# The u blocks of the experts taken in pairs, VectorE in written order, GpSimd's low part behind VectorE's

## The chip, the cores and the metric

The kernel runs on one core of one Trainium2 chip. The metric is the device time of one execution in microseconds. Before the change it is 2007.62 us, the median of 3 runs (2006.73 to 2009.07).

## The reference

Two transformer blocks on a sequence of 256 tokens of width 1024, all in float32: a gated delta net and a sliding-window attention, each with a convolutional MLP, then a block of a conformer convolution beside windowed attention, and last a product-key expert layer, which is what the change touches:

```python
def chunk_fn(hc):
    q = (hc @ w_query).reshape(TOKEN_CHUNK, PEER_HEADS, 2, PEER_HALF)
    sc = jnp.einsum('thpd,pnd->thpn', q, sub_keys).astype(jnp.float32)
    vals, idx = lax.top_k(sc, PEER_TOPK)
    cand = vals[:, :, 0, :, None] + vals[:, :, 1, None, :]
    cand_idx = idx[:, :, 0, :, None] * N_KEYS + idx[:, :, 1, None, :]
    ...
    top_s, pos = lax.top_k(cand, PEER_TOPK)
    expert_idx = jnp.take_along_axis(cand_idx, pos, axis=-1)
    gate = jax.nn.softmax(top_s, axis=-1)
    u = expert_u[expert_idx]
    act = jax.nn.gelu(jnp.einsum('thkd,td->thk', u, hc).astype(jnp.float32), approximate=False)
    vv = expert_v[expert_idx]
    return jnp.einsum('thk,thkd->td', (gate * act).astype(hc.dtype), vv)
```

There are 8 heads, 128 x 128 experts and 16 chosen experts for each head and token.

## The kernel before

The kernel doesn't gather experts. It multiplies all 16384 rows of `expert_u` with the 256 tokens, applies gelu, multiplies by a gate that is zero for experts a token did not choose, and multiplies with all of `expert_v`. The rows come in 128 blocks j of 128 rows, two of which make a pair.

One u block (L973 to L987) goes through all engines. SyncE issues four loads of 128 KB into `raw` (L976, three buffers); the rows come so arranged that VectorE's transpose by 32 x 32 squares (L978) turns the whole 128 x 1024 block into `rt` (two buffers). ScalarE rounds it to the type that TensorE multiplies at full speed: the high part `wh` (L981). The rest, `rt` - `wh`, is the low part `wl` (L223, called through `self.low`). TensorE makes 24 products of 128 x 128 by 128 x 256: for each of 8 k the high part with the tokens' high part, the high part with the tokens' low part, the low part with the tokens' high part (L239 to L241). After two blocks ScalarE writes the gelu of both (L992).

`self.low` gives a low part to VectorE (D) or GpSimd (P) by a table with a row for each stage of the kernel and a counter that runs through all of them (L85, L219 to L223): in the stage "top" the row is PPPD, in "up" PD.

The expert layer has four stages:

- **"top"**, 32 pairs (j < 64, results in `bufa`). Between them run the 8 query heads (projection and scores), the top-k of each head on VectorE (L867 to L884: MAX, MAX_INDEX, MATCH_REPLACE, the candidate sums `cand`), and the tables that turn chosen indices into key numbers and gates (L926 to L930 the selection sums `eq`, and around them).
- **"up"**, 32 pairs (j >= 64, results in `bufb`). After each pair come the gates of 8 tokens for `bufa` (L1044 to L1065): VectorE makes two pairs of one-hot operands, `ga` (L1053) and `gc` (L1056), each 128 x 512, TensorE multiplies them in 16 small products (L1062), and VectorE multiplies `bufa` by the result, which lies in PSUM (L1065). Once in 64 tokens VectorE makes the one-hot rows that `ga` and `gc` are made from (L1019 to L1040).
- **"down"** and **"last"**: the v blocks, with the gates for `bufb` in "down".

The order of instructions on each engine isn't that of the code: a scheduler, which simulates a timeline while the program is built, sets it, and each engine then works through its row in order. So in "up" VectorE's transposes, gate operands and low parts stand as the scheduler placed them.

Two helpers of the residual ahead of the expert layer matter below: `colsum` (L312 to L322), which sums squares over the rows on TensorE (L319) from the tile `rsq`, and `rcol` (L324, L328), which makes the inverse root of them on VectorE and GpSimd; `rrow` (L332 to L340) spreads that over a row tile, taken from the pool `sp`.

Of the kernel before, what the change touches and what calls it, by code (L numbers as in the profile page):

```python
# [86 lines left out]

class Net:
# [867 lines left out]
    def peer(self):  # L956
        nc, tc, I, t = self.nc, self.tc, self.I, self.t
        J0 = 64
        u_rows = I["peer_u_2"][0].rearrange("(j eb ee) (a f) -> j a ee eb f", j=P, ee=32, a=4)
        v_rows = I["peer_v_2"][0].rearrange("(j i) d -> j i d", j=P)  # L960
        xh, xl = self.pq
        tile_ = dict(reuse_waits="tile")
        with tc.tile_pool(name="ba", bufs=1, **tile_) as ba, tc.tile_pool(name="us", bufs=3, **tile_) as us, \
                tc.tile_pool(name="gp", bufs=1, **tile_) as gp, ExitStack() as late:
            bufa = t(ba, [P, J0, T], "bufa")
# [7 lines left out]
            def u_block(j, ps):  # L973
# [4 lines left out]
                nc.vector.transpose(rt, raw)  # L978
                rv = rt.rearrange("p (b f e) -> p f b e", b=4, f=DB)
                uh = t(us, [P, DB, P], "wh", F32R)  # L980
                nc.scalar.copy(uh.rearrange("p f (b e) -> p f b e", b=4), rv)  # L981
                ul = t(us, [P, DB, P], "wl", F32R)
                self.low(ul.rearrange("p f (b e) -> p f b e", b=4), rv,
                         uh.bitcast(F32).rearrange("p f (b e) -> p f b e", b=4))
                for k in range(DB):
                    self.mm3(ps, uh[:, k, :], ul[:, k, :], xh[:, k, :], xl[:, k, :], k == 0, k == DB - 1)

            def u_pair(j, buf):
                ps = self.ps("pp")
                for i in range(2):  # L990
                    u_block(j + i, ps[:, i * T : (i + 1) * T])
                nc.scalar.activation(buf[:, j % J0 : j % J0 + 2, :], ps.rearrange("p (j t) -> p j t", j=2), AF.Gelu)  # L992

            self.wide, self.nwide = True, NW[1]
# [1 line left out]
            with tc.tile_pool(name="kp", bufs=2, side="right", **tile_) as kp:  # L996
                sk = t(kp, [P, 2, P], "sk", bufs=1)
                nc.scalar.dma_start(sk, I["peer_sub_keys_2"][0].rearrange("p n d -> n p d"))
                ps = self.ps()
                for p in range(2):  # L1000
# [9 lines left out]
                          T=lambda i: self.peer_tables(kp, st, i), u=lambda j: u_pair(2 * j, bufa))  # L1010
            self.xq.close()
            bufb = t(late.enter_context(tc.tile_pool(name="bb", bufs=1, side="right", **tile_)),
                     [P, P - J0, T], "bufb")

            N = 64

            def one_hot(t0, lo):

                tk = slice(t0, t0 + N)

                def eq(out, n0, n, key):
                    nc.vector.tensor_tensor(out.rearrange("k n (g t) -> k n g t", t=4),
                                            iot[:, n0 : n0 + n].unsqueeze(2).to_broadcast([P, n, N // 4, 4]),
                                            key[:, tk].rearrange("k (g t) -> k g t", t=4).unsqueeze(1)
                                            .to_broadcast([P, n, N // 4, 4]), op=ALU.is_equal)
# [3 lines left out]
                nc.vector.tensor_tensor(a8, a8, two[:, tk].unsqueeze(1).to_broadcast([P, 8, N]), op=ALU.mult)  # L1031
# [11 lines left out]
            def gates(t0, lo, buf, bank):  # L1043


                if t0 % N == 0:
                    hot["rows"] = one_hot(t0, lo)
                a8, a16, c8, c16 = hot["rows"]
                ps = self.ps(bank)
                for t4 in (0, 4):  # L1050
                    tk = slice(t0 % N + t4, t0 % N + t4 + 4)
                    a = t(gp, [P, 8, 16, 4], "ga", BF16, bufs=2)
                    nc.vector.tensor_tensor(a, a8[:, :, tk].unsqueeze(2).to_broadcast([P, 8, 16, 4]),  # L1053
                                            a16[:, :, tk].unsqueeze(1).to_broadcast([P, 8, 16, 4]), op=ALU.mult)
                    c = t(gp, [P, 8, 16, 4], "gc", F16, bufs=2)
                    nc.vector.tensor_tensor(c, c8[:, :, tk].unsqueeze(2).to_broadcast([P, 8, 16, 4]),  # L1056
                                            c16[:, :, tk].unsqueeze(1).to_broadcast([P, 8, 16, 4]), op=ALU.mult)
                    av = a.rearrange("k h l t -> k (h l) t")
                    cv = c.rearrange("k (j g) l t -> k g j l t", g=2)
                    for i in range(4):  # L1060
                        for g in range(2):
                            nc.tensor.matmul(ps[:, (t4 + i) * 64 : (t4 + i + 1) * 64], av[:, :, i], cv[:, g, :, :, i],  # L1062
                                             start=g == 0, stop=g == 1)
                o = buf[:, :, t0 : t0 + 8]
                nc.vector.tensor_tensor(o, ps.rearrange("p (t j) -> p j t", t=8), o, op=ALU.mult)  # L1065
# [429 lines left out]
```

## Time and profile before

| what | value |
|---|---|
| median of 3 runs | 2007.62 us |
| the profiled execution | 2006.97 us |
| its span, first to last instruction | 2005.2 us |
| TensorE (PE) busy | 1867.5 us, 93% |
| VectorE (DVE) busy | 1464.4 us, 73% |
| ScalarE (ACT) busy | 958.3 us, 48% |
| GpSimd (POOL) busy | 709.2 us, 35% |
| DMA, mean | 153 GB/s |
| low parts of u blocks on GpSimd | 80, 203.2 us |
| first and last gelu of "top" start | 1143.2, 1376.1 us |
| first and last gelu of "up" start | 1381.8, 1608.6 us |

The profile is of one execution. An engine's busy time is that of its instructions, without register, branch and semaphore instructions; a busy TensorE isn't one at its peak, as its products are pipelined and overlap. In a group of instructions, out<-in are the names of tiles. The idle time that stands with an instruction or a group is that of its engine just before it, with what ended it.

### The profile page before, as it was taken

The page shows a single profiled execution, that of the slowest core. Times are in us where ns is not written, and L with a number is a line of the kernel's source. Part 1 is how long each engine was busy: PE and PEld are TensorE (multiplying, and loading weights), DVE is VectorE, ACT ScalarE, POOL GpSimd, SP SyncE. Part 2 cuts the span into 40 slices and gives each one's busy share as a digit, 9 for nine tenths or more (in the row PEclk, how much of TensorE's full clock was granted, in tenths as well). Part 3 has the DMA queues.
Part 4 walks back from the last instruction along what each step waited for, and adds up shares of the span by engine and source line. Part 5 has one row for each costly group of instructions (what it writes and reads, how often), then busy time and mean ns, then how long its engine had stood idle before and what let it go on. Part 6 is the DMA issues. An engine that isn't in the chain of part 4 may idle for free. (4 is left out here: it accounts for less than half of the span.)

```text
span 2005.2 us, 36808 instructions
## 1 busy us (share of the span) xinstructions
PE 1867.5 (93%) x14537; PEld 1760.0 (88%) x14537; DVE 1464.4 (73%) x2685; ACT 958.3 (48%) x1419; POOL 709.2 (35%) x325
## 2 busy tenths in 40 slices
PE   7879999999899999999969988799999999999998
PEld 7879999999889999989969978699989978887886
DVE  6786656766536666688854899977999977886555
ACT  5744435555555555556445434234333334344443
POOL 5444343544323444755634445454332300000000
PEclk9989999999899999999979999999999999999999
DMA  6454236566424665433535544456455545445555
GB/s 201 124 146 139 89 100 202 190 191 195 126 83 147 202 191 176 153 121 117 162 102 150 147 128 138 119 159 174 137 147 138 148 147 167 159 160 172 194 194 173
DMA packets 243434, 306.29 MB, mean 153 GB/s; under 512 B 26076, under 2 KB 213821, under 8 KB 243133
## 3 DMA queue, kind: packets, MB, share of 16 engines
q1 hardware_dynamic: 240864, 302.84, 49.2%
q8 instruction: 114, 1.87, 0.4%
q10 hardware_dynamic: 2237, 1.07, 0.2%
q14 instruction: 59, 0.48, 0.1%
q0 software_dynamic: 160, 0.02, 0.0%
HBM read 298.60 MB, written 4.74 MB: 151 GB/s over the span
## 5 line engine op out<-in xcount | busy, mean ns | idle before, releaser
L223 POOL TENSOR_TENSOR wl<-raw,wh 128x1024 fp32r<-128x1024 f32 (+1 forms) x196 | 470.7, 2405 | 555.0 <-ACT wh L232 506.9
L232 ACT CAST wh<-raw 128x1024 fp32r<-128x1024 f32 (+1 forms) x285 | 297.8, 1048 | 322.2 <-issue 108.9
L239 PE MATMUL pa<-xh,wh 128*128 128x256 f32 (+1 forms) x1336 | 388.8, 291 | 26.9 <-ACT wh L981 17.8
L239 PE MATMUL pp<-xh,wh 128*128 128x256 f32 x1392 | 395.5, 284 | 16.6 <-DVE kq L481 9.8
L241 PE MATMUL pp<-xh,wl 128*128 128x256 f32 x1392 | 394.3, 283 | 4.1 <-DVE wl L223 2.6
L241 PE MATMUL pa<-xh,wl 128*128 128x256 f32 (+1 forms) x1336 | 386.8, 291 | 11.0 <-DVE wl L223 7.6
L240 PE MATMUL pp<-xl,wh 128*128 128x256 f32 x1392 | 393.1, 282 | 2.1 <-DVE xl L364 2.1
L240 PE MATMUL pa<-xl,wh 128*128 128x256 f32 (+1 forms) x1336 | 385.3, 289 | 1.6 <-DVE xl L364 1.5
L223 DVE TENSOR_TENSOR wl<-raw,wh 128x1024 fp32r<-128x1024 f32 x233 | 296.8, 1274 | 112.3 <-ACT wh L232 55.8
L223 POOL TENSOR_TENSOR wl<-rt,wh 128x1024 fp32r<-128x1024 f32 x80 | 203.2, 2546 | 272.4 <-ACT wh L981 258.9
L239 PEld LDWEIGHTS pa<-xh,wh 128*128 128x128 f32 (+1 forms) x1336 | 262.3, 197 | 32.2 <-ACT wh L981 21.6
L239 PEld LDWEIGHTS pp<-xh,wh 128*128 128x128 f32 x1392 | 266.9, 192 | 18.8 <-issue 10.2
L241 PEld LDWEIGHTS pa<-xh,wl 128*128 128x128 f32 (+1 forms) x1336 | 262.1, 197 | 13.7 <-DVE wl L223 8.7
L241 PEld LDWEIGHTS pp<-xh,wl 128*128 128x128 f32 x1392 | 266.8, 192 | 6.1 <-DVE wl L223 3.7
L240 PEld LDWEIGHTS pp<-xl,wh 128*128 128x128 f32 x1392 | 267.1, 192 | 2.5 <-DVE xl L364 2.3
L240 PEld LDWEIGHTS pa<-xl,wh 128*128 128x128 f32 (+1 forms) x1336 | 262.1, 196 | 3.0 <-DVE xl L364 1.9
L981 ACT CAST wh<-rt 128x1024 fp32r<-128x1024 f32 x128 | 133.9, 1049 | 223.1 <-DVE rt L978 204.3
L1086 PE MATMUL pa<-wh,rt 128*128 128x512 f32 x512 | 200.9, 394 | 0.0
L1085 PE MATMUL pa<-wl,rt 128*128 128x512 f32 x512 | 200.3, 391 | 0.0
L1076 ACT CAST wh<-raw 128x1024 fp32r<-128x1024 f32 x128 | 134.5, 1051 | 108.6 <-PE pa L1086 97.3
L978 DVE STREAM_TRANSPOSE rt<-raw 128x1024 f32<-128x1024 f32 x128 | 156.3, 1229 | 16.9 <-POOL wl L223 16.6
L1084 PE MATMUL pa<-wh,rt 128*128 128x512 f32 x512 | 161.4, 393 | 1.4 <-ACT rt L1070 1.4
(422 smaller groups left out, 3450.2 us busy)
## 6 DMA issues: line engine op xcount, KB each, us to landing
raw<-in_peer_u_dram SPq DMA_DIRECT2D x512, 128.0 KB
raw<-in_peer_v_dram SPq DMA_DIRECT2D x128, 512.0 KB
raw<-in_ffn_w_up_dram SPq DMA_DIRECT2D x88, 512.0 KB
raw<-in_a_w_in_dram SPq DMA_DIRECT2D x48, 512.0 KB
raw<-in_ffn_w_down_dram SPq DMA_DIRECT2D x44, 512.0 KB
raw<-in_w_in_dram SPq DMA_DIRECT2D x44, 512.0 KB
raw<-in_a_w_out_dram SPq DMA_DIRECT2D x16, 512.0 KB
raw<-in_peer_w_query_dram SPq DMA_DIRECT2D x16, 512.0 KB
```

The costliest lines, as they stand in the source:

```text
L223: (self.nc.vector if order[self.turn % len(order)] == "D" else self.nc.gpsimd).tensor_tensor(out, raw, high, op=ALU.subtract)
L232: nc.scalar.copy(wh, raw)
L239: mm(out, wh, xh, start=start, stop=False, skip_group_check=skip)
L240: mm(out, wh, xl, start=False, stop=False, skip_group_check=skip)
L241: mm(out, wl, xh, start=False, stop=stop, skip_group_check=skip)
L978: nc.vector.transpose(rt, raw)
L981: nc.scalar.copy(uh.rearrange("p f (b e) -> p f b e", b=4), rv)
L1076: nc.scalar.copy(vh, raw)
L1084: nc.tensor.matmul(o, w2[:, 0, i, s], vh[:, c], start=first, stop=False)
L1085: nc.tensor.matmul(o, w2[:, 0, i, s], vl[:, c], start=False, stop=False)
L1086: nc.tensor.matmul(o, w2[:, 1, i, s], vh[:, c], start=False, stop=last)
```

## The change

The function for one u block becomes two: `u_turned` loads a block, transposes it and makes its high part; `u_pair` does this for j + 1 (b) and then for j (a), calls `between` if there is one, and then makes both low parts: VectorE that of b, GpSimd that of a. Before the low parts VectorE copies one column of b's high part into the buffer of a's low part; GpSimd's low part overwrites that, and so waits for it. TensorE takes b first, then a. The table and counter no longer decide for u blocks.

In "up" everything that VectorE does for pairs and gates goes through `InOrder`, which makes the scheduler keep the order of the code. `between` multiplies the `bufa` columns of the pair before by its gates (`gated`) and then makes this pair's gate operands and products. In "top" VectorE's order is still the scheduler's. `rt` has three buffers where it had two, in the v pairs too. The row tile of `rrow` comes from the pool `cp`, again with two buffers.

```diff
+class InOrder:
...
+    def __getattr__(self, name):
+        f = getattr(self.eng, name)
+        return lambda *a, **kw: self.tc.keep_in_program_order(f(*a, **kw))
...
-        row = self.t(pool or self.sp, [P, T], tag)
+        row = self.t(pool or self.cp, [P, T], tag, **({} if pool else dict(bufs=2)))
...
+            ve = [nc.vector]
...
-                rt = t(us, [P, D], "rt", bufs=2)
-                nc.vector.transpose(rt, raw)
+                rt = t(us, [P, D], "rt", bufs=3)
+                ve[0].transpose(rt, raw)
...
-                ul = t(us, [P, DB, P], "wl", F32R)
-                self.low(ul.rearrange("p f (b e) -> p f b e", b=4), rv,
-                         uh.bitcast(F32).rearrange("p f (b e) -> p f b e", b=4))
-                for k in range(DB):
-                    self.mm3(ps, uh[:, k, :], ul[:, k, :], xh[:, k, :], xl[:, k, :], k == 0, k == DB - 1)
-
-            def u_pair(j, buf):
+                return rv, uh
+
+            def u_pair(j, buf, between=None):
                 ps = self.ps("pp")
-                for i in range(2):
-                    u_block(j + i, ps[:, i * T : (i + 1) * T])
+                rb, bh = u_turned(j + 1)
+                ra, ah = u_turned(j)
+                al, bl = t(us, [P, DB, P], "wl", F32R), t(us, [P, DB, P], "wl", F32R)
+                if between:
+                    between()
+
+                ve[0].tensor_copy(al[:, 0, 0:1], bh[:, 0, 0:1])
+                for eng, lo, high, rv in ((ve[0], bl, bh, rb), (nc.gpsimd, al, ah, ra)):
+                    eng.tensor_tensor(lo.rearrange("p f (b e) -> p f b e", b=4), rv,
+                                      high.bitcast(F32).rearrange("p f (b e) -> p f b e", b=4), op=ALU.subtract)
+                for i, uh, ul in ((1, bh, bl), (0, ah, al)):
+                    for k in range(DB):
+                        self.mm3(ps[:, i * T : (i + 1) * T], uh[:, k, :], ul[:, k, :], xh[:, k, :], xl[:, k, :],
+                                 k == 0, k == DB - 1)
                 nc.scalar.activation(buf[:, j % J0 : j % J0 + 2, :], ps.rearrange("p (j t) -> p j t", j=2), AF.Gelu)
...
             self.stage = "up"
+            made = []
+
+            def between(t0):
+
+                if made:
+                    gated(made.pop())
+                made.append(gates(t0, 0, bufa, "pm"))
+
+            ve[0] = InOrder(tc, nc.vector)
             for j in range(J0, P, 2):
-                u_pair(j, bufb)
-                gates(4 * (j - J0), 0, bufa, "pm")
+                u_pair(j, bufb, lambda: between(4 * (j - J0)))
+            gated(made.pop())
+            ve[0] = nc.vector
```

How the order of instructions changes, at three places (the number of the row on its engine, the line, the operation, out<-in, the shape).

VectorE in "up", somewhat more than one pair before: `rt` is the turned block, `wl` the low part, `bufa` the gated product.

```order
1643 L978 STREAM_TRANSPOSE rt_16710<-raw_16705 128x1024
1644 L1053 TENSOR_TENSOR ga_16679<-a_2205_16569,a_2206_16570 128x512
1645 L1056 TENSOR_TENSOR gc_16681<-c_2208_16575,c_2209_16576 128x512
1646 L223 TENSOR_TENSOR wl_16651<-rt_16647,wh_16649 128x1024
1647 L1065 TENSOR_TENSOR bufa_12354<-pm_16580,bufa_12354 128x64x8
1648 L1053 TENSOR_TENSOR ga_16691<-a_2205_16569,a_2206_16570 128x512
1649 L1056 TENSOR_TENSOR gc_16693<-c_2208_16575,c_2209_16576 128x512
1650 L978 STREAM_TRANSPOSE rt_16745<-raw_16740 128x1024
1651 L1053 TENSOR_TENSOR ga_16777<-a_2205_16569,a_2206_16570 128x512
1652 L1056 TENSOR_TENSOR gc_16779<-c_2208_16575,c_2209_16576 128x512
1653 L978 STREAM_TRANSPOSE rt_16808<-raw_16803 128x1024
1654 L1065 TENSOR_TENSOR bufa_12354<-pm_16678,bufa_12354 128x64x8
```

VectorE in "up", one pair after; rows that `InOrder` issues all have its line, L95, and the COPY is the one-column copy.

```order
1698 L95 STREAM_TRANSPOSE rt_16443<-raw_16438 128x1024
1699 L95 STREAM_TRANSPOSE rt_16452<-raw_16447 128x1024
1700 L95 TENSOR_TENSOR bufa_12354<-pm_16360,bufa_12354 128x64x8
1701 L95 TENSOR_TENSOR ga_16460<-a_2088_15755,a_2089_15756 128x512
1702 L95 TENSOR_TENSOR gc_16462<-c_2091_15761,c_2092_15762 128x512
1703 L95 TENSOR_TENSOR ga_16472<-a_2088_15755,a_2089_15756 128x512
1704 L95 TENSOR_TENSOR gc_16474<-c_2091_15761,c_2092_15762 128x512
1705 L95 COPY wl_16456<-wh_16445 128x1
1706 L95 TENSOR_TENSOR wl_16457<-rt_16443,wh_16445 128x1024
```

Before, transposes, gate operands and low parts alternate, and nothing says where GpSimd is meanwhile. After, every pair has the same nine rows, with the copy right ahead of VectorE's low part and the gated product and the four gate operands between the transposes and the copy.

VectorE in "top", at the top-k of one of the last heads, before: `cand` are its candidate sums, `tops` and `pos` what it chose.

```order
1384 L869 MATCH_REPLACE cand_13099<-tops_12374,cand_13099 128x136
1385 L869 MATCH_REPLACE cand_13117<-tops_12374,cand_13117 128x136
1386 L870 MAX tops_12374<-cand_13099 128x8
1387 L870 MAX tops_12374<-cand_13117 128x8
1388 L978 STREAM_TRANSPOSE rt_14190<-raw_14185 128x1024
1389 L871 MAX_INDEX pos_12375<-tops_12374,cand_13099 128x8
1390 L223 TENSOR_TENSOR wl_14157<-rt_14153,wh_14155 128x1024
1391 L871 MAX_INDEX pos_12375<-tops_12374,cand_13117 128x8
1392 L882 TENSOR_TENSOR cand_13206<-vals_12372 128x16
```

And at the same head after; the copy has line L1007, the low part L1009.

```order
1427 L991 STREAM_TRANSPOSE rt_14283<-raw_14278 128x1024
1428 L877 MAX tops_12374<-cand_13099 128x8
1429 L877 MAX tops_12374<-cand_13117 128x8
1430 L878 MAX_INDEX pos_12375<-tops_12374,cand_13099 128x8
1431 L991 STREAM_TRANSPOSE rt_14347<-raw_14342 128x1024
1432 L878 MAX_INDEX pos_12375<-tops_12374,cand_13117 128x8
1433 L1007 COPY wl_14287<-wh_14276 128x1
1434 L879 MATCH_REPLACE cand_13099<-tops_12374,cand_13099 128x136
1435 L879 MATCH_REPLACE cand_13117<-tops_12374,cand_13117 128x136
1436 L1009 TENSOR_TENSOR wl_14288<-rt_14274,wh_14276 128x1024
```

One low part of VectorE for four transposes became one for two, and between the copy and the low part other instructions stand (two MATCH_REPLACE here). The last selection sum of top-k (L930 before, L940 after) stands behind 44 of the 64 transposes of "top" before, and behind 57 of them after.

TensorE ahead of "top", before: `pa_12376` and `pa_12483` are the first query heads, `rsq` the squares of the residual, `hT` its columns.

```order
7187 L240 MATMUL pa_12376<-xl_12218,wh_12409 128x256
7188 L241 MATMUL pa_12376<-xh_12217,wl_12411 128x256
7189 L239 MATMUL pa_12376<-xh_12217,wh_12409 128x256
7190 L319 MATMUL pm_12260<-ones_85,rsq_12219 128x1 x4
7191 L816 MATMUL pm_12270<-c_head_81,hT_83 128x128 x4
7192 L240 MATMUL pa_12376<-xl_12218,wh_12409 128x256
```

And after.

```order
7133 L251 MATMUL pa_11713<-xh_11708,wl_12164 128x256
7134 L249 MATMUL pa_12376<-xh_12217,wh_12379 128x256
7135 L250 MATMUL pa_12376<-xl_12218,wh_12379 128x256
7136 L329 MATMUL pm_12260<-ones_85,rsq_12219 128x1 x4
7137 L826 MATMUL pm_12270<-c_head_81,hT_83 128x128 x4
7138 L251 MATMUL pa_12376<-xh_12217,wl_12381 128x256
7139 L249 MATMUL pa_12376<-xh_12217,wh_12379 128x256
```

Before, 56 products of the two heads stand ahead of the column sum (L319); after, two do (L329), and the rest follow.

More of the change, by code (lines that the diff above doesn't have):

```diff
@@ L85, with __init__ @@
 LOW = dict(gdn="PPD", ffn="PD", swa="PPD", mix="P", tail="PPD", top="PPPD", up="PD", down="D", last="D")
+class InOrder:
+    def __init__(self, tc, eng):
+        self.tc, self.eng = tc, eng
+    def __getattr__(self, name):
+        f = getattr(self.eng, name)
+        return lambda *a, **kw: self.tc.keep_in_program_order(f(*a, **kw))
 class Net:
@@ L971, in peer, with u_turned @@
             nc.vector.tensor_copy(iot, self.iota[:, 0:16].unsqueeze(2).to_broadcast([P, 16, 4]))
-            def u_block(j, ps):
+            ve = [nc.vector]
+            def u_turned(j):
                 raw = t(us, [P, D], "raw")
@@ L1023, in eq @@
                 def eq(out, n0, n, key):
-                    nc.vector.tensor_tensor(out.rearrange("k n (g t) -> k n g t", t=4),
+                    ve[0].tensor_tensor(out.rearrange("k n (g t) -> k n g t", t=4),
                                             iot[:, n0 : n0 + n].unsqueeze(2).to_broadcast([P, n, N // 4, 4]),
@@ L1030, in one_hot @@
                 eq(a8, 0, 8, part[:, 0, 1])
-                nc.vector.tensor_tensor(a8, a8, two[:, tk].unsqueeze(1).to_broadcast([P, 8, N]), op=ALU.mult)
+                ve[0].tensor_tensor(a8, a8, two[:, tk].unsqueeze(1).to_broadcast([P, 8, N]), op=ALU.mult)
                 eq(a16, 0, 16, part[:, 1, 1])
@@ L1035, in one_hot @@
                 eq(h4, lo // 16, 4, part[:, 0, 0])
-                nc.vector.tensor_tensor(c8, h4.unsqueeze(2).to_broadcast([P, 4, 2, N]),
+                ve[0].tensor_tensor(c8, h4.unsqueeze(2).to_broadcast([P, 4, 2, N]),
                                         gate[:, :, tk].unsqueeze(1).to_broadcast([P, 4, 2, N]), op=ALU.mult)
@@ L1052, in gates @@
                     a = t(gp, [P, 8, 16, 4], "ga", BF16, bufs=2)
-                    nc.vector.tensor_tensor(a, a8[:, :, tk].unsqueeze(2).to_broadcast([P, 8, 16, 4]),
+                    ve[0].tensor_tensor(a, a8[:, :, tk].unsqueeze(2).to_broadcast([P, 8, 16, 4]),
                                             a16[:, :, tk].unsqueeze(1).to_broadcast([P, 8, 16, 4]), op=ALU.mult)
                     c = t(gp, [P, 8, 16, 4], "gc", F16, bufs=2)
-                    nc.vector.tensor_tensor(c, c8[:, :, tk].unsqueeze(2).to_broadcast([P, 8, 16, 4]),
+                    ve[0].tensor_tensor(c, c8[:, :, tk].unsqueeze(2).to_broadcast([P, 8, 16, 4]),
                                             c16[:, :, tk].unsqueeze(1).to_broadcast([P, 8, 16, 4]), op=ALU.mult)
@@ L1063, in gates, with gated @@
                                              start=g == 0, stop=g == 1)
+                return ps, t0, buf
+            def gated(g):
+                ps, t0, buf = g
                 o = buf[:, :, t0 : t0 + 8]
-                nc.vector.tensor_tensor(o, ps.rearrange("p (t j) -> p j t", t=8), o, op=ALU.mult)
+                ve[0].tensor_tensor(o, ps.rearrange("p (t j) -> p j t", t=8), o, op=ALU.mult)
             def v_pair(j, w):
-                w2 = t(us, [P, 2, 2, T], "rt", F32R, bufs=2)
+                w2 = t(us, [P, 2, 2, T], "rt", F32R, bufs=3)
                 nc.scalar.copy(w2[:, 0], w)
@@ L1095, in peer @@
                 v_pair(j, bufa[:, j : j + 2, :])
-                gates(4 * j, J0, bufb, "pm")
+                gated(gates(4 * j, J0, bufb, "pm"))
             self.stage = "last"
```

## The prediction

> **What bounds the kernel now.** I read the busy shares first, then the busy time stage by stage, then the stage that the change rewrites.
>
> ```profile
> span 2005.2 us, 36808 instructions
> PE 1867.5 (93%) x14537; PEld 1760.0 (88%) x14537; DVE 1464.4 (73%) x2685; ACT 958.3 (48%) x1419; POOL 709.2 (35%) x325
> ```
>
> Over the span TensorE is the bound. The windows show where it isn't (columns: the stretch, its length, then PE, PEld, VectorE, ScalarE and GpSimd busy, granted clock, DMA share, GB/s):
>
> ```profile
> 1200.00:1300.00 100.00, 81.87 (x582) 77.05 (x582) 100.00 (x183) 35.00 (x42) 47.23 (x18) 0.91 0.44 128
> 1300.00:1400.00 100.00, 95.33 (x803) 93.75 (x803) 74.95 (x80) 41.73 (x47) 53.91 (x22) 0.97 0.61 169
> 1400.00:1500.00 100.00, 94.08 (x864) 92.10 (x864) 99.48 (x119) 35.63 (x41) 32.42 (x13) 0.98 0.50 138
> 1500.00:1600.00 100.00, 91.96 (x857) 89.17 (x856) 99.31 (x116) 34.42 (x40) 34.91 (x14) 1.00 0.53 144
> 1600.00:1700.00 100.00, 98.40 (x619) 81.47 (x618) 80.39 (x132) 40.99 (x48) 1.21 (x1) 0.98 0.47 155
> ```
>
> From 1200 to 1300 and from 1400 to 1600 VectorE is full and TensorE isn't; from 1600 on TensorE is full and GpSimd has no work, so what is saved ahead of 1600 reaches the end. The gelu that closes each pair of u blocks gives the pace (min/median/max duration in ns, then first and last start):
>
> ```profile
> L992 ACT ACTIVATE bufa<-pa x21: 590/599/602, 1151.6 to 1376.1; 128x512 f32<-128x512 f32 x21
> L992 ACT ACTIVATE bufb<-pp x11: 587/597/600, 1388.5 to 1608.6; 128x512 f32<-128x512 f32 x11
> 1353.49 0.60 ACT L992 ACTIVATE bufa<-pp 128x512 f32<-128x512 f32 x1 [1.89 <-PE pp L241]
> 1370.45 0.60 ACT L992 ACTIVATE bufa<-pp 128x512 f32<-128x512 f32 x1 [1.85 <-PE pp L241]
> ```
>
> The 32 pairs of the stage "up" end between 1376.1 and 1608.6: 232.5 us, 7.27 a pair. At the end of "top", where no gates run, three pairs take 1370.45 - 1353.49 = 16.96, 5.65 each: TensorE's own pace for 48 u products. With gates it shows this:
>
> ```profile
> 1460.79 0.66 PE L1062 MATMUL pm<-gc,ga 128*128 128x64 f16 x8
> 1464.16 0.65 PE L1062 MATMUL pm<-gc,ga 128*128 128x64 f16 x8
> 1467.54 0.66 PE L1062 MATMUL pm<-gc,ga 128*128 128x64 f16 x8
> ```
>
> From one group of eight gate products to the next, with 24 u products between, lie 3.37 and 3.38 us: 6.75 a pair. So TensorE loses 0.52 us a pair in "up", and VectorE is what it waits for. Why VectorE is slow stands in its groups from 1400 to 1605 (count | busy us, mean ns | idle before):
>
> ```profile
> L978 DVE STREAM_TRANSPOSE rt<-raw 128x1024 f32<-128x1024 f32 x54 | 65.8, 1229 | 0.2
> L1053 DVE TENSOR_TENSOR ga<-a,a 128x512 bf16<-128x512 bf16 x55 | 46.3, 844 | 0.3 <-PE pm L1062 0.3
> L1056 DVE TENSOR_TENSOR gc<-c,c 128x512 f16<-128x512 f16 x56 | 45.2, 807 | 0.0
> L223 DVE TENSOR_TENSOR wl<-rt,wh 128x1024 fp32r<-128x1024 f32 x28 | 38.0, 1356 | 0.3 <-ACT wh L981 0.3
> L1065 DVE TENSOR_TENSOR bufa<-pm,bufa 128x512 f32<-128x512 f32 x28 | 18.6, 665 | 0.5 <-PE pm L1062 0.5
> ```
>
> Beside them stand single instructions of VectorE, and the two of GpSimd that run meanwhile (start, duration):
>
> ```profile
> 1440.21 0.68 DVE L1065 TENSOR_TENSOR bufa<-pm,bufa 128x512 f32<-128x512 f32 x1
> 1440.81 2.01 DVE L1053 TENSOR_TENSOR ga<-a,a 128x512 bf16<-128x512 bf16 x1
> ...
> 1446.57 0.69 DVE L1065 TENSOR_TENSOR bufa<-pm,bufa 128x512 f32<-128x512 f32 x1 [0.45 <-PE pm L1062]
> 1447.18 0.42 DVE L1053 TENSOR_TENSOR ga<-a,a 128x512 bf16<-128x512 bf16 x1
> 1447.51 0.42 DVE L1056 TENSOR_TENSOR gc<-c,c 128x512 f16<-128x512 f16 x1
> 1447.85 3.42 DVE L223 TENSOR_TENSOR wl<-rt,wh 128x1024 fp32r<-128x1024 f32 x1
> ...
> 1481.29 1.21 DVE L223 TENSOR_TENSOR wl<-rt,wh 128x1024 fp32r<-128x1024 f32 x1
> 1482.42 2.36 DVE L978 STREAM_TRANSPOSE rt<-raw 128x1024 f32<-128x1024 f32 x2
> 1484.71 0.65 DVE L1065 TENSOR_TENSOR bufa<-pm,bufa 128x512 f32<-128x512 f32 x1
> ...
> 1487.83 1.02 DVE L1024 TENSOR_TENSOR a<-iot,part 128x512 bf16<-128x512 bf16 x2
> ...
> 1490.04 1.22 DVE L223 TENSOR_TENSOR wl<-rt,wh 128x1024 fp32r<-128x1024 f32 x1
> ```
>
> ```profile
> 1439.67 2.88 POOL L223 TENSOR_TENSOR wl<-rt,wh 128x1024 fp32r<-128x1024 f32 x1 [2.93 <-ACT wh L981]
> 1447.68 2.51 POOL L223 TENSOR_TENSOR wl<-rt,wh 128x1024 fp32r<-128x1024 f32 x1 [5.13 <-ACT wh L981]
> ```
>
> The ga at 1440.81 lies under GpSimd's low part of 1439.67 and ends with it: 2.01 us, where a free one takes 0.42 (1447.18). VectorE's low part of 1447.85 began 0.17 after GpSimd's and took 3.42 instead of 1.21 (1481.29). The product at 1440.21, one operand of which lies in PSUM, isn't lengthened, and the mean of 54 transposes is 1229 ns. The surplus in 1400 to 1605 is (46.3 - 55 x 0.42) + (45.2 - 56 x 0.42) + (38.0 - 28 x 1.21) = 23 + 22 + 4 = 49 us of 205. It goes the other way too: GpSimd's 2.88 (1439.67) against 2.51 (1447.68) has the end of a VectorE low part in it.
>
> **The change in "up".** VectorE's row for a pair becomes two transposes, the product of the pair before, ga, gc, ga, gc, the one-column copy, its low part. GpSimd's low part waits for the copy, so it comes to the port as VectorE enters its own. It waits that one out (1.1 us) and then needs 2.5 (1447.68) beside two transposes and the product, which GpSimd wasn't seen to lengthen and which last 2.9 (below): it is through 0.4 us before the next ga. Start to start: two transposes 1484.71 - 1482.42 = 2.29; the product 0.61 (1446.57 to 1447.18); four gate operands 2 x 0.67 (1447.18 to 1447.85); the low part 1.13 (1481.29 to 1482.42): 5.37. The copy isn't in this trace; it costs between 0 and 0.16 (the two-column instruction at 1084.18, quoted below), I take 0.1, near that row. The one-hot rows come once in eight pairs, 1490.04 - 1487.83 = 2.2, a fraction of a us more for a product that stands apart: 0.3 a pair. Sum 5.8 us, under TensorE's 6.75. So TensorE becomes the bound: 32 x 6.75 = 216, and 2 for filling at the start and the four lumps of one-hot rows: 218 for 232.5, **-14.5**. Bounds: 7.0 a pair (224, -6 with the 2) if half of today's loss stays; 6.6 (211, -21) if the sixteen gate products, which now stand together, cost only their busy time over 5.65 (0.65 + 0.66 less overlap).
>
> The waits that the change adds: VectorE's copy waits for ScalarE's high part of block b, with the low part and the next transposes queued behind it; it stands behind four gate operands and a product (1.95 us) after the second transpose:
>
> ```profile
> L981 ACT CAST wh<-rt 128x1024 fp32r<-128x1024 f32 x128 | 133.9, 1049 | 223.1 <-DVE rt L978 204.3
> ```
>
> The high part takes 1.05 us, so it is covered; without that cover each pair would lose up to 1.05. VectorE's low part always goes into the same buffer, which TensorE leaves when it has done the last pair's b; a's 24 products and the gates (3.4 us and more) then cover 1.2 us of low part. Two transposes in a row need both raw blocks; the second's load starts when the first of the pair before is through, 6.75 us ahead. Two blocks in 6.75 us are 155 GB/s, and 1300 to 1400 had 169. The third buffer of rt only takes waits away.
>
> **The change in "top".** GpSimd had three of four low parts (48), VectorE 16; now each has 32. VectorE gains 16 x 1.13 = 18 us and 32 copies, 3; it loses gate work that ran here before and now belongs to "up" (six ga, as many gc, a set of one-hot rows: 4.6 + 4.6 + 2.4 = 12). That is +9. Contention in "top" shows in these groups (1112 to 1376):
>
> ```profile
> L926 DVE TENSOR_TENSOR eq<-abf,io 128x512 bf16<-128x512 bf16 x16 | 23.6, 1487 | 0.0
> L1053 DVE TENSOR_TENSOR ga<-a,a 128x512 bf16<-128x512 bf16 x6 | 4.6, 780 | 0.0
> ```
>
> At 0.42 each the 16 eq alone lose 17. Sixteen fewer GpSimd low parts give back between 7 and 28 (0.4 to 49 / 28 = 1.75 each). But here other instructions, often top-k ones of half a us to several us, stand between the copy and VectorE's low part, so GpSimd may be first, and the low part waits the rest of 2.5 us: 0 to 32 us for 16 more of them at up to 2.0. I take these as even, **0** (-15 to +25). On the other side, VectorE idles 25 us from 1300 to 1400, where top-k is over and TensorE sets the pace. In the new order the last selection of top-k stands behind 57 of 64 transposes, where it stood behind 44, so most of that idle time gets work: -15 (0 to -25). "Top": +9 + 0 - 15 = **-6** (-21 to +19).
>
> **Ahead of "top".** The residual's row tile moves to another pool, and the order shifts around it.
>
> ```profile
> 1067.43 2.87 DVE L223 TENSOR_TENSOR wl<-raw,wh 128x1024 fp32r<-128x1024 f32 x1
> ...
> 1077.41 0.69 DVE L292 TENSOR_TENSOR rsq<-pm,rsq 128x512 f32<-128x512 f32 x1 [0.31 <-ACT pm L291]
> 1084.18 0.16 DVE L328 TENSOR_SCALAR rcol<-pm 128x2 f32<-128x2 f32 x1 [6.08 <-PE pm L319]
> ```
>
> ```profile
> 1073.83 0.58 PE L239 MATMUL pa<-xh,wh 128*128 128x256 f32 x1 [2.96 <-ACT hT L294]
> 1075.00:1080.00 5.00, 5.00 (x27) 5.00 (x26) 2.60 (x5) 2.90 (x7) 0.00 (x0) 0.53 0.06 14
> ```
>
> TensorE did its column sum only when 56 products of the first query heads were through, so rcol came 6 us after rsq was ready (1078.1). Now the sum stands behind two of them and TensorE waits for rsq, about 4 us, after an idle time that already left it at clock 0.53; the low part of 1067.43 no longer stands between the residual's adds, which brings rsq up to 2.9 us forward. Between -3 and +4; **+1.5**, as the deferred products have to be done anyway. By the Trainium skill, "TensorE: Matmul & The Clock Gate", Part 1, the half clock comes after an idle window of about 3.4 us; here 2.96 sufficed.
>
> **Sum.** -14.5 - 6 + 1.5 = -19. The profiled run took 2006.97 us (span 2005.2 and 1.8 around it), so 1988; it lies 0.65 under the median of the runs, so **1988.5**. No change means within 0.2%, 4 us, about what a measurement here can tell.
>
> **Rivals.**
> - *GpSimd wins the lock in "up"* (slower). The copy ends, its semaphore frees GpSimd, and GpSimd's read starts before VectorE's low part. Then each low part costs 3.42 as at 1447.85, 2.2 more: 5.8 + 2.2 = 8.0 a pair, 258 in all, +25; with -6 and +1.5 about 2028. It decides where the gap on VectorE between copy and low part exceeds the semaphore's way. For it: a lead of 0.17 us sufficed at 1447.68. Against: the two stand side by side, and while TensorE is the bound GpSimd waits longer for a's high part. 0.10. The Trainium skill, "SBUF — State Buffer", Who interferes with whom, has it as a rule that issue order decides who blocks, in an exclusive lock of the shared ports; by it alone this case would follow wherever GpSimd's instruction goes out first, with 2028 for 1988.5. The rows at 1439.67 and 1447.68 agree on the lock, one for each order; no run here shows yet who goes out first behind such a copy.
> - *"Top" is blocked*: its upper end, +19, with -14.5 and +1.5: about 2013. VectorE is full there, so each blocked low part counts. 0.09.
> - *"Up" stays at its pace*, since something else holds TensorE, such as loads in pairs: only -4.5, about 2003. Against: the 49 us of surplus, and the 169 GB/s. 0.08.
> - *Both ends low*: "top" -21, "up" -21: about 1967. 0.09.
>
> The forecast itself has 0.64, from 1975 to 2002. The range reaches down to 1970 and up to 2012, which leaves out the first rival, half of the second and most of the last. Faster: 0.64 + 0.09 + half of 0.08 = 0.77; same 0.07 (the other half, and cases of the second that come out even); slower 0.16.
>
> **What would show it.** In the new profile: "up" gelus 6.6 to 7.0 us apart; ga and gc at about 420 ns mean and VectorE's low parts near 1.2 us there; VectorE below 90% busy from 1400 to 1580 and TensorE at 98%; the last gelu of "top" near 1371. Low parts of 3.4 us in "up" prove the first rival; in "top" alone, the second. ga and gc free but a pace above 7 would prove the third and my reading of the bound wrong.

## The result and the profile after

The changed kernel takes 1988.78 us, the median of 6 runs (1984.17 to 1991.49); before it were 2007.05 (6 runs, 2003.16 to 2009.07). The ratio is 0.9908, 95% interval 0.9894 to 0.9922: 18 us faster, where 1988.5 had been forecast. The profiled run took 1986.34 us. The page of after:

```profile
span 1984.6 us, 36930 instructions
PE 1848.3 (93%) x14537; PEld 1747.2 (88%) x14537; DVE 1438.0 (72%) x2765; ACT 956.5 (48%) x1419; POOL 671.8 (34%) x309
```

The windows of after, with the columns of before:

```profile
1200.00:1300.00 100.00, 78.73 (x647) 76.02 (x646) 100.00 (x182) 38.61 (x46) 34.53 (x14) 1.00 0.54 145
1300.00:1400.00 100.00, 92.80 (x768) 91.65 (x769) 94.26 (x139) 37.09 (x43) 38.31 (x14) 0.95 0.57 151
1400.00:1500.00 100.00, 100.00 (x959) 99.35 (x958) 88.23 (x148) 38.76 (x46) 38.72 (x15) 1.00 0.57 159
1500.00:1600.00 100.00, 100.00 (x912) 97.42 (x912) 86.72 (x141) 41.39 (x49) 34.33 (x13) 1.00 0.52 152
```

From 1400 to 1600 TensorE and VectorE have changed places: TensorE 100% where it was 94 and 92, VectorE 88 and 87 where it was 99. From 1200 to 1300 the bound is as before: VectorE is full and TensorE short of work. The gelus (duration min/median/max, first and last start):

```profile
L1015 ACT ACTIVATE bufa<-pa x21: 589/590/602, 1152.2 to 1375.5; 128x512 f32<-128x512 f32 x21
L1015 ACT ACTIVATE bufb<-pa x21: 582/601/604, 1382.2 to 1583.8; 128x512 f32<-128x512 f32 x21
L1015 ACT ACTIVATE bufa<-pp x11: 585/590/597, 1144.2 to 1370.7; 128x512 f32<-128x512 f32 x11
L1015 ACT ACTIVATE bufb<-pp x11: 585/600/604, 1388.8 to 1590.5; 128x512 f32<-128x512 f32 x11
```

"Top" ends at 1375.5 (before 1376.1), "up" takes 1590.5 - 1375.5 = 215.0 (before 232.5), 6.72 a pair. From there to the end of the span are 394.1 us, 396.6 before. So of 20.6 us between the two profiles "up" gave 17.5, "top" 0.6, and 2.5 lie in the stages behind.

Why "up" is faster shows in VectorE's groups of after, 1400 to 1580 (L95 is what `InOrder` issues):

```profile
L95 DVE STREAM_TRANSPOSE rt<-raw 128x1024 f32<-128x1024 f32 x54 | 63.8, 1220 | 0.0
L95 DVE TENSOR_TENSOR wl<-rt,wh 128x1024 fp32r<-128x1024 f32 x27 | 33.0, 1223 | 15.4 <-PE pa L251 10.3 <-PE pp L251 5.1
L95 DVE TENSOR_TENSOR gc<-c,c 128x512 f16<-128x512 f16 x54 | 22.6, 419 | 0.0
L95 DVE TENSOR_TENSOR ga<-a,a 128x512 bf16<-128x512 bf16 x54 | 22.5, 417 | 0.0
```

`ga` went from 844 ns to 417, `gc` from 807 to 419, the low part from 1356 to 1223. The low part now has idle time ahead of it, ended by TensorE: VectorE waits for TensorE, not TensorE for it. One pair, VectorE first and GpSimd behind:

```profile
1464.08 0.42 DVE L95 TENSOR_TENSOR ga<-a,a 128x512 bf16<-128x512 bf16 x1
...
1465.42 0.15 DVE L95 CAST wl<-wh 128x1 fp32r<-128x1 f32 x1
1466.36 1.22 DVE L95 TENSOR_TENSOR wl<-rt,wh 128x1024 fp32r<-128x1024 f32 x1 [0.79 <-PE pp L251]
1467.50 2.36 DVE L95 STREAM_TRANSPOSE rt<-raw 128x1024 f32<-128x1024 f32 x2
```

```profile
1460.76 2.40 POOL L1009 TENSOR_TENSOR wl<-rt,wh 128x1024 fp32r<-128x1024 f32 x1 [4.29 <-ACT wh L994]
1467.46 2.41 POOL L1009 TENSOR_TENSOR wl<-rt,wh 128x1024 fp32r<-128x1024 f32 x1 [4.30 <-ACT wh L994]
```

GpSimd's 2.4 us begin as VectorE's low part ends and lie under the two transposes. But what released GpSimd isn't the copy, 2 us earlier: it is ScalarE's high part of a, which itself mostly waits until TensorE leaves a buffer. So it is for 27 of GpSimd's 32 low parts from 1374 to 1582; four waited for the copy. That put a question to the theory of the prediction: is the copy needed at all? And "top" asked another: why did it gain nothing?

### The profile page after: what moved, and what is told of

It reads as the page before. It is cut to its first block, busy times and chain, and to the rows that moved or that the text cites. A ratio compares the mean times of both kernels' runs of the same rounds, so it can differ in the third digit from the quotient of the medians.

```text
span 1984.6 us, 36930 instructions
## 1 busy us (share of the span) xinstructions
PE 1848.3 (93%) x14537; PEld 1747.2 (88%) x14537; DVE 1438.0 (72%) x2765; ACT 956.5 (48%) x1419; POOL 671.8 (34%) x309
## 5 line engine op out<-in xcount | busy, mean ns | idle before, releaser
L251 PE MATMUL pa<-xh,wl 128*128 128x256 f32 (+1 forms) x1336 | 382.0, 286 | 19.7 <-DVE wl L1009 19.6
L249 PE MATMUL pa<-xh,wh 128*128 128x256 f32 (+1 forms) x1336 | 382.9, 287 | 14.4 <-ACT hT L304 6.2
L250 PE MATMUL pa<-xl,wh 128*128 128x256 f32 (+1 forms) x1336 | 381.1, 285 | 2.0 <-DVE xl L374 1.9
L251 PEld LDWEIGHTS pa<-xh,wl 128*128 128x128 f32 (+1 forms) x1336 | 257.3, 193 | 22.4 <-DVE wl L1009 22.4
L249 PEld LDWEIGHTS pa<-xh,wh 128*128 128x128 f32 (+1 forms) x1336 | 257.3, 193 | 16.5 <-ACT hT L304 6.6
L1009 POOL TENSOR_TENSOR wl<-rt,wh 128x1024 fp32r<-128x1024 f32 x64 | 166.0, 2594 | 291.1 <-ACT wh L994 209.2
L250 PEld LDWEIGHTS pa<-xl,wh 128*128 128x128 f32 (+1 forms) x1336 | 257.3, 193 | 3.2 <-DVE xl L374 2.4
```

Source lines behind the costliest of these rows:

```text
L249: mm(out, wh, xh, start=start, stop=False, skip_group_check=skip)
L250: mm(out, wh, xl, start=False, stop=False, skip_group_check=skip)
L251: mm(out, wl, xh, start=False, stop=stop, skip_group_check=skip)
L1009: eng.tensor_tensor(lo.rearrange("p f (b e) -> p f b e", b=4), rv, high.bitcast(F32).rearrange("p f (b e) -> p f b e", b=4), op=ALU.subtract)
```

## The experiments

All ratios are to the kernel before. "Top" is the start of its last gelu, "up" the time from there to the last gelu of "up", both from the one profiled run; runs of one kernel spread by 3 to 13 us, so these are read to a few us. The profiled run is the fastest of ten (2002.2 us) for the scheduler's order in "up" and the fastest of nine (2007.4) for "top" alone, 7 us under their medians. The column "top" counts from the start of the span, so it takes in what lies ahead: the first gelu of "top" starts at 1143.2 before, 1144.2 in the change and 1144.1 to 1151.8 in the others.

| kernel | median us | ratio, 95% interval | top | up |
|---|---|---|---|---|
| before | 2007 | | 1376.1 | 232.5 |
| the change | 1988.8 | 0.9908 (0.9894 to 0.9922) | 1375.5 | 215.0 |
| without the copy | 1993.5 | 0.9920 (0.9893 to 0.9946) | 1360.9 | 238.6 |
| scheduler's order in "up" | 2008.8 | 1.0008 (0.9993 to 1.0023) | 1381.4 | 227.2 |
| "up" alone | 1969.2 | 0.9808 (0.9781 to 0.9834) | 1358.2 | 215.0 |
| copy behind the low part | 1965.4 | 0.9774 (0.9747 to 0.9802) | 1358.8 | 215.9 |
| third buffer alone | 1997.4 | 0.9942 (0.9923 to 0.9961) | 1370.5 | 230.8 |
| "up" alone, two buffers | 1996.7 | 0.9944 (0.9927 to 0.9962) | 1375.8 | 224.5 |
| "top" alone | 2014.4 | 1.0046 (1.0026 to 1.0066) | 1379.2 | 229.1 |
| the change, two buffers | 1981.9 | 0.9875 (0.9838 to 0.9913) | 1367.4 | 223.9 |
| copy behind, three to one | 1981.4 | 0.9874 (0.9840 to 0.9907) | 1372.0 | 216.0 |

**Without the copy.**

```diff
-                ve[0].tensor_copy(al[:, 0, 0:1], bh[:, 0, 0:1])
```

> The changed kernel without the one-column copy, so that GpSimd's low part waits only for ScalarE's high part of a. Theory A, the hold is what frees the gate operands: without it GpSimd starts under ga and gc, whose mean goes from 0.42 us back towards 0.8, 'up' takes 7.2 us a pair and the time is about 2005. Theory B, the written order and the buffers do it: while TensorE is the bound, a's high part waits for a buffer that TensorE leaves just as VectorE's low part starts, so GpSimd cannot be early; 'up' stays at 6.7 us a pair, ga and gc at 0.42, and the time is 1985 to 1992.

"Up" went to 7.3 us a pair (1381.2 to 1599.5 for 30 of them), as theory A has it, but by another instruction than it named, and the time, 1993.5, lies between the two theories. The start of "up" runs as theory B says; then come VectorE's one-hot rows, and this, VectorE and GpSimd of this kernel:

```profile
1409.57 1.22 DVE L95 TENSOR_TENSOR wl<-rt,wh 128x1024 fp32r<-128x1024 f32 x1
...
1418.59 2.60 DVE L95 TENSOR_TENSOR gc<-c,c 128x512 f16<-128x512 f16 x1
...
1426.45 3.42 DVE L95 TENSOR_TENSOR wl<-rt,wh 128x1024 fp32r<-128x1024 f32 x1
```

```profile
1411.61 2.40 POOL L1008 TENSOR_TENSOR wl<-rt,wh 128x1024 fp32r<-128x1024 f32 x1 [4.29 <-ACT wh L994]
1418.31 2.60 POOL L1008 TENSOR_TENSOR wl<-rt,wh 128x1024 fp32r<-128x1024 f32 x1 [4.30 <-ACT wh L994]
1426.40 2.40 POOL L1008 TENSOR_TENSOR wl<-rt,wh 128x1024 fp32r<-128x1024 f32 x1 [5.48 <-ACT wh L994]
```

At 1418 VectorE is late by the one-hot rows, so GpSimd starts under `gc` (2.60 us). At 1426.40 it leads VectorE's low part by 0.05 us, and that takes 3.42. From 1426 to 1531 twelve of fifteen low parts are blocked like that and VectorE is busy 104.4 us of 105; from 1543 on none is, so the pairs can come back without a copy too, but late. In the change the same lump of one-hot rows ends so (VectorE, then GpSimd):

```profile
1427.92 0.14 DVE L95 CAST wl<-wh 128x1 fp32r<-128x1 f32 x1
1427.98 1.21 DVE L95 TENSOR_TENSOR wl<-rt,wh 128x1024 fp32r<-128x1024 f32 x1
```

```profile
1428.23 3.24 POOL L1009 TENSOR_TENSOR wl<-rt,wh 128x1024 fp32r<-128x1024 f32 x1 [5.21 <-DVE wl L95]
```

Here the copy releases GpSimd, VectorE's low part is out 0.25 us ahead of it, and it is GpSimd that waits (3.24 us for 2.40). So while TensorE is the bound the copy does nothing, and after a disturbance it keeps VectorE's low part first. In pace that is worth 30 x (7.28 - 6.72) = 17 us; the rest of the 23.6 is the start of "up", whose first pairs here wait for the last tables of "top" (first gelu of "up" at 1380.7). That "top" ends at 1360.9 here doesn't show that the copy costs 14.6 us there. VectorE's low parts in it are blocked as in the change (60.6 us for 32, where the change has 58.8), and the work on the tables, over at 1361.7 in the change, goes on to 1380.7 here, beyond the end of "top". By the second gelu of "up" the lead is 7.6 us (1381.2 against 1388.8); what the copy costs in "top" stays open. In the whole, the change is 4.7 us faster than this kernel by the medians, less than the two intervals can tell apart.

**The scheduler's order in "up".**

```diff
-            ve[0] = InOrder(tc, nc.vector)
```

> The changed kernel with VectorE's order in 'up' left to the scheduler; pairs, split and copy as in the change. Theory A, the hold suffices wherever the operations stand: 'up' 6.7 to 6.8 us a pair, 1987 to 1993. Theory B, the written order is needed, since the scheduler puts gate operands behind the copy or behind VectorE's low part, where GpSimd's 2.4 us block them: ga and gc at a mean of 0.6 to 0.8 us, 'up' at 7.0 to 7.3 us a pair, 1999 to 2008.

Theory B, a little beyond its time: no gain is left (ratio 1.0008). From 1400 to 1560 `ga` has a mean of 698 ns and VectorE's low part 1782; `gc`, which the theory named too, stays at 413. The low part is the larger share, and one place in VectorE's order shows how: the copy stands ahead of a transpose here, GpSimd gets in between and VectorE's low part waits for it. VectorE and GpSimd of this kernel:

```profile
1453.03 0.14 DVE L1007 CAST wl<-wh 128x1 fp32r<-128x1 f32 x1
1453.10 1.23 DVE L991 STREAM_TRANSPOSE rt<-raw 128x1024 f32<-128x1024 f32 x1
1454.25 3.42 DVE L1009 TENSOR_TENSOR wl<-rt,wh 128x1024 fp32r<-128x1024 f32 x1
```

```profile
1454.18 2.41 POOL L1009 TENSOR_TENSOR wl<-rt,wh 128x1024 fp32r<-128x1024 f32 x1 [2.96 <-ACT wh L994]
```

A lead of 0.07 us cost 2.2. The first rival of the prediction is a real mechanism; in the changed "up" TensorE's pace keeps it out of most pairs, and the copy's place right ahead of the low part out of those behind one-hot rows.

**"Up" alone.** "Top" is made block by block again, with the table and no copy:

```diff
-                self.play(PEER, ..., u=lambda j: u_pair(2 * j, bufa))
+                self.play(PEER, ..., u=lambda j: u_old(2 * j, bufa))
```

> The change in 'up' alone: in 'top' each block is made as before, with the table PPPD for its low part and without a copy. Theory A, as the prediction had it: 'top' is worth 6 us of the gain, so this takes 6 us more than the change, 1993 to 1997. Theory B, as the new trace reads: the last gelu of 'top' starts at 1375.5 where it was 1376.1, so 'top' gained nothing and this is even with the change, 1986 to 1991.

Neither: it is some 20 us faster than the whole change. "Up" is the same to a tenth (215.0), and "top" ends at 1358.2. So the changed "top" doesn't just gain nothing: beside the other parts of the change it loses 17 us that they had gained.

**The copy behind VectorE's low part**, so that GpSimd waits until that is done:

```diff
-                ve[0].tensor_copy(al[:, 0, 0:1], bh[:, 0, 0:1])
                 for eng, lo, high, rv in ((ve[0], bl, bh, rb), (nc.gpsimd, al, ah, ra)):
+                    if eng is nc.gpsimd:
+                        ve[0].tensor_copy(al[:, 0, 0:1], bl[:, 0, 0:1])
```

> The changed kernel with the one-column copy taken from VectorE's low part of b and not from its high part, so that GpSimd's low part waits until VectorE's own is done. Theory A, 'top' is bound by VectorE and its low parts wait behind GpSimd's (mean 1.84 us for 1.21, 32 of them, 20 us): they come down to about 1.25 us, other operations with two inputs are blocked somewhat more, 'top' ends 8 to 18 us earlier, 1971 to 1981. Theory B, the lock is only moved to the candidate sums and selections, or TensorE sets the pace of 'top' as it is: 1986 to 1992. 'Up' stays at 6.7 us a pair in both.

Theory A, and beyond its time: "top" ends 16.7 us earlier, and the whole, 1965.4, beats both kernels. First the change, VectorE and GpSimd in "top":

```profile
1213.49 0.14 DVE L1007 CAST wl<-wh 128x1 fp32r<-128x1 f32 x1
1213.96 3.39 DVE L1009 TENSOR_TENSOR wl<-rt,wh 128x1024 fp32r<-128x1024 f32 x1
1221.03 0.13 DVE L1007 CAST wl<-wh 128x1 fp32r<-128x1 f32 x1
1221.62 3.27 DVE L1009 TENSOR_TENSOR wl<-rt,wh 128x1024 fp32r<-128x1024 f32 x1
```

```profile
1213.88 2.40 POOL L1009 TENSOR_TENSOR wl<-rt,wh 128x1024 fp32r<-128x1024 f32 x1 [5.15 <-DVE tops L877]
1221.41 2.40 POOL L1009 TENSOR_TENSOR wl<-rt,wh 128x1024 fp32r<-128x1024 f32 x1 [5.14 <-ACT wh L994]
```

Top-k instructions stand between copy and low part, 0.47 to 0.59 us in all; GpSimd starts 0.4 us after the copy, ahead of the low part. Ten of the 32 low parts of "top" took 2.5 to 3.4 us. Then the groups of low parts in "top" (1112 to 1376) in the change, and (1112 to 1350) with the copy behind:

```profile
L1009 DVE TENSOR_TENSOR wl<-rt,wh 128x1024 fp32r<-128x1024 f32 x32 | 58.8, 1838 | 3.6 <-PE pp L251 3.6
```

```profile
L1010 DVE TENSOR_TENSOR wl<-rt,wh 128x1024 fp32r<-128x1024 f32 x32 | 42.1, 1316 | 0.1
```

58.8 - 42.1 = 16.7 us, as much as "top" ends earlier; other groups moved by a few us either way (the candidate sums from 8.9 to 6.1, the first selection sums from 12.4 to 14.3).

**The third buffer alone**, in the kernel before:

```diff
-                rt = t(us, [P, D], "rt", bufs=2)
+                rt = t(us, [P, D], "rt", bufs=3)
...
-                w2 = t(us, [P, 2, 2, T], "rt", F32R, bufs=2)
+                w2 = t(us, [P, 2, 2, T], "rt", F32R, bufs=3)
...
-        row = self.t(pool or self.sp, [P, T], tag)
+        row = self.t(pool or self.cp, [P, T], tag, **({} if pool else dict(bufs=2)))
```

> The kernel before with one part of the change alone: three buffers for the turned block, and the row tile in the other pool, which makes the room for it. Theory A, the third buffer is what moves 'top': the last selection then stands behind 59 of 64 transposes (44 before), VectorE's idle time from 1300 to 1400 gets work and 'top' ends 10 to 18 us earlier; 'up' keeps 7.1 to 7.3 us a pair; 1988 to 1998. Theory B, the third buffer only takes waits away that cost nothing: 2003 to 2009.

Theory A with a smaller size: 10 us in the whole (ratio 0.9942), and in the profile 5.6 up to the end of "top" and 1.7 in "up". Transposes that waited 16.6 us in "top" for GpSimd's low parts no longer do, but low parts of VectorE now meet GpSimd's more often: 16 of them at a mean of 1.64 us (1112 to 1360), where it was 1.34.

**"Up" alone with two buffers:** the kernel of 1969.2 us with `bufs=2` at both places.

> The change in 'up' alone, as in the run that took 1969 us, but with two buffers for the turned block. Theory A, the third buffer carries the gain of 'top' there, and is needed in 'up' too, since a's transposes would wait for GpSimd's low part: 'top' ends at 1366 to 1376 and 'up' takes 6.9 to 7.2 us a pair, 1990 to 2002. Theory B, the 18 us of 'top' come from the gate work that the written order moves to 'up', not from the buffer, and TensorE still bounds 'up': 1966 to 1975.

Theory A. "Up" takes 7.0 us a pair, and the transposes there show the wait (1400 to 1560):

```profile
L95 DVE STREAM_TRANSPOSE rt<-raw 128x1024 f32<-128x1024 f32 x46 | 57.3, 1246 | 24.2 <-POOL wl L1009 23.4
```

"Top" ends at 1375.8, as before, though less gate work stands ahead of that. So moving it away is worth nothing with two buffers. With three, "up" alone ends "top" 1370.5 - 1358.2 = 12.3 us ahead of the third buffer alone; VectorE's rows for gates ahead of that end fall from 14.3 to 5.5 us, and what the other 3.5 are wasn't traced.

**"Top" alone:** the pairs and the copy in "top", `u_old` and the gates behind it in "up", without `InOrder`.

> The changed 'top' alone (pairs, copy, low parts one to one, three buffers), 'up' block by block as before with the scheduler's order. Theory A, the pairs of 'top' as changed cost what the third buffer brings: 'top' ends at 1373 to 1385 and 'up' takes 7.0 to 7.3 us a pair, 2000 to 2010. Theory B, the changed 'top' is a gain by itself and was only hidden: 1985 to 1998.

Theory A, and beyond its time: 2014.4, slower than before by 0.46% (0.26 to 0.66). "Top" ends at 1379.2, though three buffers alone had brought it to 1370.5.

**The change with two buffers.**

```diff
-                rt = t(us, [P, D], "rt", bufs=3)
+                rt = t(us, [P, D], "rt", bufs=2)
...
-                w2 = t(us, [P, 2, 2, T], "rt", F32R, bufs=3)
+                w2 = t(us, [P, 2, 2, T], "rt", F32R, bufs=2)
```

> The whole change but with two buffers for the turned block. Theory A, the third buffer is needed in both stages: 'top' ends 5 to 15 us later than in the change and 'up' goes to 6.9 to 7.2 us a pair, because a's transpose waits for GpSimd's low part of the pair before; 2000 to 2015. Theory B, it isn't: 1986 to 1992.

Theory A fell for "top", which ends at 1367.4, and held for "up" (223.9, 8.9 us more than the change). The median is 7 us under that of the change, but the two intervals overlap. With two buffers the scheduler put copy and low part closer (1207.76 and 1207.81, 1212.99 and 1213.33), and VectorE's low parts are free:

```profile
L1009 DVE TENSOR_TENSOR wl<-rt,wh 128x1024 fp32r<-128x1024 f32 x32 | 38.8, 1213 | 4.9 <-PE pa L251 3.2 <-PE pp L251 1.7
```

The distance between those two rows isn't all: the last four low parts (from 1341.95 on) start 0.95 us behind the copy and are free too, since GpSimd waited still longer for ScalarE's high part. Nothing in the code sets either time in "top". And of the 20 us that the low parts gained, "top" kept 8: the first selection sums (L936) took 23.1 us for 12.4, and the transposes waited 7.4 for buffers.

**The copy behind, three low parts to one:** in every second pair of "top" GpSimd makes both low parts, without a copy.

```diff
+                both = self.stage == "top" and j % 4 == 0
-                for eng, lo, high, rv in ((ve[0], bl, bh, rb), (nc.gpsimd, al, ah, ra)):
-                    if eng is nc.gpsimd:
+                for eng, lo, high, rv in ((nc.gpsimd if both else ve[0], bl, bh, rb), (nc.gpsimd, al, ah, ra)):
+                    if eng is nc.gpsimd and not both:
```

> As the run with the copy behind VectorE's low part, but in every second pair of 'top' GpSimd makes both low parts and there is no copy, so GpSimd has 48 and VectorE 16 of them there, as before the change. Theory A, 'top' is bound by VectorE's work: 16 low parts and copies less are 20 us, of which the lock takes a part back from the selections and candidate sums; 'top' ends 4 to 12 us earlier than 1358.8, 1953 to 1962. Theory B, what VectorE saves in work it loses behind GpSimd's 16 more low parts, or TensorE, 90% busy there, sets the end: 'top' ends at 1354 to 1364, 1962 to 1971.

Both theories missed: "top" ends at 1372.0, 13 us later than one to one. GpSimd's low parts come three in a row (7.1 to 8.0 us). The transposes wait for their buffers and the candidate sums for GpSimd (1112 to 1376):

```profile
L991 DVE STREAM_TRANSPOSE rt<-raw 128x1024 f32<-128x1024 f32 x64 | 78.3, 1230 | 11.0 <-POOL wl L1011 11.0
...
L892 DVE TENSOR_TENSOR cand<-vals 128x16 f32<-128x16 f32 x16 | 17.8, 1115 | 0.0
```

With one to one the sums had a mean of 383 ns (6.1 us), and the transposes no such wait. The 20 us of work taken from VectorE were paid back there and in the selection sums (34.2 us in all for 25.8).

## Why the prediction was right, and where only its sum was

**What bounds "up", and its -14.5.** Right: 215.0 was measured for 218, 6.72 us a pair for 6.75. The sizes hold too: `ga`, `gc` and the low part at 0.42, 0.42 and 1.22, VectorE at 87 to 88%. The 2 us for filling and the one-hot lumps were not needed: they disappear in the slack of 0.8 us a pair. The copy lasts 0.15 us, and the next instruction starts 0.06 after it where nothing else holds that up (1427.92, 1427.98); 0.1 was taken from bounds of 0 and 0.16.

**GpSimd "waits for the copy".** Half right. In the steady state it waits for a's high part; the copy acts after a disturbance. Who goes out first behind it, which the prediction left open, is settled where the two stand side by side: VectorE, by 0.25 us (1427.98, 1428.23). The run without the copy shows that it is still worth 17 us of pace. The written order is needed as well: without it nothing was left of the gain.

**The waits that the change adds** were covered as said: no idle time stands before the copy. The step that the third buffer "only takes waits away" was too small a view of it: in "up" it is worth 9.5 us (224.5 against 215.0), which the prediction's sum used without naming it.

**"Top", -6.** This step failed in its terms. The last gelu of "top" moved by -0.6, and 1.0 of that is the later start, so "top" itself gained 1.6 for 6. The prediction had +9 of work, 0 of contention and -15 of idle time filled. The two traces give the terms (1112 to 1376, the windows and VectorE's groups, before and then after):

```profile
1112.00:1376.00 264.00, 230.16 (x1765) 221.63 (x1764) 241.35 (x621) 101.08 (x125) 130.97 (x52) 0.94 0.50 142
L223 DVE TENSOR_TENSOR wl<-rt,wh 128x1024 fp32r<-128x1024 f32 x17 | 22.7, 1337 | 6.0 <-ACT wh L981 6.0
L1056 DVE TENSOR_TENSOR gc<-c,c 128x512 f16<-128x512 f16 x6 | 2.4, 415 | 0.0
```

```profile
1112.00:1376.00 264.00, 219.87 (x1746) 213.57 (x1746) 260.02 (x638) 100.44 (x123) 92.09 (x37) 0.97 0.54 142
L936 DVE TENSOR_TENSOR eq<-abf,io 128x512 bf16<-128x512 bf16 x16 | 12.4, 810 | 0.0
```

- Idle time filled: VectorE idled 22.7 us before and 4.0 after, -19 for -15. This term held.
- Work: about +15 for +9. The low parts and copies are as counted. But the six `gc` were put at 4.6 us, like `ga`, and took 2.4; and a set of one-hot rows and four gate operands, 4.5 us, still stand ahead of the end of "top". So about 6 us of gate work left "top", not 12.
- Contention: about +7 for 0. The low parts take 20 us more than 1.21 each (58.8 for 32), where it was 2 more (22.7 for 17), so +18, a little over half of the "0 to 32 us" that the prediction saw coming. The first selection sums gave back 11 of that (12.4 for 23.6); the other groups nearly cancel.

Top-k instructions of some 4 us that had moved ahead of 1112 make up the rest. The second rival was therefore at work, at well under its price (the terms give some +7 of contention for the +25 of its upper end): GpSimd first where other instructions stand between copy and low part, as the rows at 1213 and 1221 show. The run with the copy behind the low part took 16.7 us of it out.

The runs by parts give another sum to the same -0.6: the third buffer -5.6, the written "up" beside it -12.3, the pairs with their copy in "top" +17.3. These aren't prices that a part has by itself. With two buffers the same pairs bring the end of "top" from 1375.8 to 1367.4, -8.4, and the third buffer then costs 8.1. The scheduler's order differs with each edit, and which of its differences counts wasn't separated.

That the sum fits as well as it does, -20.6 between the profiles for -19, is in part luck: 3 us more than forecast in "up" and 2.5 behind it make up for the 4 that "top" and what lies ahead of it fell short.

**Ahead of "top", +1.5.** The first gelu of "top" starts at 1144.2 where it was 1143.2: 1.0. Only the size held. VectorE and TensorE of after:

```profile
1073.87 0.69 DVE L302 TENSOR_TENSOR rsq<-pm,rsq 128x512 f32<-128x512 f32 x1 [1.25 <-ACT pm L301]
...
1076.79 0.15 DVE L338 TENSOR_SCALAR rcol<-pm 128x2 f32<-128x2 f32 x1
```

```profile
1073.40 0.58 PE L249 MATMUL pa<-xh,wh 128*128 128x256 f32 x1 [4.99 <-ACT wh L855]
...
1074.61 1.86 PE L329 MATMUL pm<-ones,rsq 128*128 128x1 f32 x8 [0.42 <-DVE rsq L302]
```

`rsq` came 3.5 us earlier and `rcol` 7.4, and TensorE idled 4.99 us in a row where it had idled 2.96. But it didn't idle for `rsq`, as the step had it: for that it waited 0.42 us. The 4.99 end with ScalarE's high part of the query weights (L855), which ScalarE starts only at 1072.28, behind instructions of the residual. That the two sides nearly cancel came out; why TensorE would wait did not.

**Open.** 2.5 us of the 20.6 lie behind "up", in stages whose work didn't change. From the last gelu of "up" to the end the profiles of all these kernels take 391 to 397 us, with and without the third buffer; no run was made for it.

## What to carry to other kernels

Where two engines block each other as here, the one that is out first goes through and the other waits the whole of it out. So what decides is which two instructions meet, and not only how much work each has. Hold the slow engine by something that the fast one makes right beside its own conflicting instruction, and fix that order in the code. Where a scheduler may put half a microsecond between, the hold can come undone, and something made right behind, from that instruction's output, is safer: in "top" it was worth 16.7 us, in the written order of "up" nothing (215.9 for 215.0). And test the parts of a change alone, also where the forecast fits: here two stages with opposite signs added up to it, and leaving one part out gained as much again as the whole. Such tests don't give a part one price: the pairs in "top" cost 17.3 us beside three buffers and saved 8.4 beside two.

## What the runs showed of the hardware

A lead of 0.05 to 0.08 us of GpSimd was enough to cost VectorE's low part 2.2 us (1426.40, 1454.18, 1213.88), and VectorE's low part of 1134.82, 0.01 ahead of GpSimd's, went through in 1.21 while that took 3.45: who is first is settled within a tenth of a microsecond, and the loser waits out the whole. The hundredths aren't to be read: at 1356.82 VectorE's went through in 1.22 too, and there GpSimd's record (3.49 us) begins 0.01 ahead. TensorE's granted clock stayed at 1.00 in the window 1200 to 1300 of the change although it was busy only 79%, where before it was 0.91 at 82%. The single idle times listed there are 1.6 to 2.3 us in the change and 0.3 to 2.1 before; what made the difference wasn't tried.
